# Laying the weight matrices of a one-step decoder out in the order of their transfers

## The chip, the cores and the metric

The kernel runs on one NeuronCore of one Trainium2 chip. The metric is the device time of one execution in microseconds (us), as the median of several runs. A second number, the span, is the time from the first to the last instruction in the one execution that was taken with the hardware profiler; that execution has a time of its own, which is given beside its span below.

The engines have short names throughout: PE is TensorE (its matmuls), PEld is TensorE's weight loading, DVE is VectorE, ACT is ScalarE, POOL is GpSimd, SP is SyncE. SP and POOL issue the transfers here; "SPq" is the time in which SP issues one. All transfers run on the core's 16 DMA engines.

## The reference

One step of a decoder layer for 256 prompt positions and 8 x 4 sampled positions, 288 columns in all, with a model width of 2048 and a feed-forward width of 5632, all in float32. Cut to what is computed:

```python
def ffn_half(h, g, wg, wu, wd):
    hn = rms_norm(h, g)
    return h + 0.5 * ((jax.nn.silu(hn @ wg) * (hn @ wu)) @ wd)

hp = ffn_half(hp, norm_ffn1, w_ffn1_gate, w_ffn1_up, w_ffn1_down)
cb, u, q, k, v, logf = mixer_in(hp, norm_mix, w_in, b_f)      # one projection of 6152 columns
conv_y = cb * short_conv(u_ext, conv_w)
attn_o = fox_prompt(q, k, v, logf)                            # causal, with forget gates
hp = mixer_out(hp, conv_y, attn_o, norm_conv_out, norm_attn_out, w_out)
hp = ffn_half(hp, norm_ffn2, w_ffn2_gate, w_ffn2_up, w_ffn2_down)
hp = ple_add(hp, p_prompt, norm_ple, w_ple_gate, w_ple_proj)
y_prompt = rms_norm(hp, norm_final)
```

The sampled positions go through the same layer, except that their attention (`fox_sample`) also reads 1024 past keys, values and forget gates of each of 8 sequences through a page table. The last 8 columns of `w_in` are the forget-gate weights.

## The kernel before, in words

**Weights.** Every large matrix is used in tiles of 512 rows by 256 columns (256 rows in a few down projections and in `w_ple_proj`). A tile of 512 rows is four blocks of 128 rows; row r of each block lies on partition r, so a partition holds four runs of 256 float32 (1 KB each) of one tile. `weight` (L270) names such a tile as a slice of the matrix, and `load_upto` (L237) issues its transfer on SP's queue (L242) into one of `RAW = 8` buffers of the pool `rawp`. The same eight buffers also take the pages of cached values, which POOL gathers (L250). `split_upto` (L257) then cuts a tile into halves of two blocks and splits each into a high and a low part: ACT writes `whi` (L265), DVE subtracts it to give `wlo` (L266), and there are `HALVES = 5` buffers of each. `pair` (L276) multiplies: for each block and each of two groups of 128 columns there are three matmuls (L298 to L300) with 288 moving columns. A half is therefore 12 matmuls, a tile 24.

**Order.** `steps` is a list of (transfers, function) that `run_steps` (L312) works off: before each step the loads of the next eight items are issued, then the function emits its instructions. Each engine executes what it was given in that order. A transfer on SP's queue waits, on SP, for its buffer to be released and for the eighth transfer before it on that queue to land, since eight semaphores are used in turn; everything behind it on SP waits with it.

**Small loads.** `small_loads` (L161, issued at L166) puts four transfers on SP's queue in the middle of the first feed-forward layer, behind seven loads of gains (L137): the forget-gate bias `bf`, the forget-gate weights `wf`, and the page table in two forms, `pidx` and `ptb`. `wf` is `w_in[:, 6144:6152]`: 2048 runs of 8 float32 (32 bytes). From `ptb`, DVE makes `idx` (L167), the row numbers for all gathers. Behind them on SP come the next weight tiles.

**Keys and values.** `k_turn` (L461, with `k_fetch` L456) gathers one page of keys with POOL (`kg`, L458), transposes it on DVE (`kt`, L467) and stores it with POOL to DRAM (`KD`, L469); 64 pages are spread over the first feed-forward layer. During the mixer, `k_scores` reads them back (`KT<-KD`, L247) and multiplies (L726). `v_round` gathers four pages of values for each of 16 rounds (L250) and multiplies them (L783). `prompt_head` (L822) has POOL load a row of forget sums, `bk`, and wait for it before its next instruction (L824).

Of the kernel before, what the change touches and what calls it, by code (L numbers as in the profile page):

```python
# [25 lines left out]
P = 128  # L26
D = 2048
KT = D // P
# [6 lines left out]
NH = 8  # L35
# [53 lines left out]
def build(nc, tc, ctx, A, O):  # L89
# [3 lines left out]
    v, s, g, pe, sy = nc.vector, nc.scalar, nc.gpsimd, nc.tensor, nc.sync  # L93
# [23 lines left out]
    cols = A["consts"].shape[1]  # L117
# [3 lines left out]
    def const(name):  # L121
        r, a, b = CONST_COLS[name]
        return C[:r, a:b]
# [32 lines left out]
    wf = cst.tile([P, KT, NH], F32, name="wf")  # L156
# [3 lines left out]

    def small_loads():  # L161
        for to, src in ((bf, A["b_f"].rearrange("(h o) -> h o", o=1)),
                        (wf, A["w_in"][:, 6144:6152].rearrange("(k p) c -> p k c", p=P)),
                        (pidx, A["page_table"].rearrange("b (g o) -> (b g) o", o=1)),
                        (ptb, A["page_table"].rearrange("b g -> (b g)").partition_broadcast(P))):
            tc.keep_in_program_order(sy.dma_start(to, src))  # L166
        v.tensor_scalar(idx, ptb, float(P), const("iota"), ALU.mult, ALU.add)  # L167
# [69 lines left out]
    def load_upto(n):  # L237
        while state["loaded"] < min(n, len(items)):
            it = items[state["loaded"]]
            if it["kind"] == "w":  # L240
                t = rawp.tile([P, it["nk"], 256], F32, name="wraw", tag="raw")
                d = sy.dma_start(t, it["src"].rearrange("(k p) c -> p k c", p=P))  # L242
                if state["used"] < 24:
                    tc.keep_in_program_order(d)
            elif it["kind"] == "k":
                t = W["kt"][0].tile([P, 2, 4, NH, 32], F32, name="KT", tag="KT", bufs=3)
                sy.dma_start(t.rearrange("p a i h r -> p (a i h r)"), it["src"])  # L247
            else:
                t = rawp.tile([P, NH * P], F32, name="page", tag="raw")
                g.indirect_dma_start(out=t, out_offset=None, in_=it["src"],  # L250
                                     in_offset=bass.IndirectOffsetOnAxis(ap=it["rows"], axis=0))
            it["tile"] = t
            state["loaded"] += 1
# [14 lines left out]
            state["split"] += 1  # L268

    def weight(src, k0, nk, c0):  # L270
        return dict(kind="w", src=src[k0 * P:(k0 + nk) * P, c0:c0 + 256], nk=nk, parts={})

    def page(src, j):
        return dict(kind="p", src=src, rows=idx[:, j:j + 1])
# [1 line left out]
    def pair(src, c0, kts, act, evac, k_of=lambda k: k, late=0, tag="mm"):  # L276
# [4 lines left out]
        for ci, ks in enumerate(chunks):  # L281
            it = weight(src, ks[0], len(ks), c0)

            def fn(ci=ci, ks=ks, it=it):
                if ci == 0:
                    st["ps"] = [bank(tag, BANKS[tag]) for _ in range(2)]
                last = ci == len(chunks) - 1
                split_upto(state["halves_used"] + HALVES)
                state["chunk"] += 1
                for b in range(2):  # L290
                    o = st["ps"][b][:, :NT]
                    for j, k in enumerate(ks):
                        hi, lo = it["parts"][j // 2 * 2]
                        w = slice(b * P, b * P + P)
                        xh, xl = act(k_of(k))
                        f = ci == 0 and j == 0
                        l = last and j == len(ks) - 1
                        pe.matmul(o, hi[:, j % 2, w], xh, start=f, stop=False)  # L298
                        pe.matmul(o, hi[:, j % 2, w], xl, start=False, stop=False)  # L299
                        pe.matmul(o, lo[:, j % 2, w], xh, start=False, stop=l)  # L300
                    if b == 0:
                        run_deferred()
                    if last and late:
                        defer(lambda b=b, o=o: evac(b, o), late)
                    elif last:
                        evac(b, o)
                state["halves_used"] += len(ks) // 2

            out.append(([it], fn))
        return out  # L310

    def run_steps():  # L312
        for its, _ in steps:
            items.extend(its)
            for it in its:
                if it["kind"] == "w":
                    halves.extend((it, j) for j in range(0, it["nk"], 2))
        for its, fn in steps:
            load_upto(state["used"] + RAW)
            fn()  # L320
            state["used"] += len(its)
# [150 lines left out]
    def later_loads():  # L472
        t = load_gains(["norm_mix", "norm_ffn2", "norm_ple", "norm_final", "norm_conv_out", "norm_attn_out", "conv_w"], 16, sy)
        small_loads()
        defer(lambda: turn_gains(*t), 20)
# [17 lines left out]
    for c in range(4):  # L493
        xin.append(x_load(2 * c))
        xin.append(x_load(2 * c + 1))
        load_upto(c + 1)
# [662 lines left out]
]  # L1159


# [19 lines left out]
```

## Time and profile before

| | us |
|---|---|
| median of 3 runs | 2389.52 |
| lowest, highest | 2389.41, 2391.86 |
| the profiled execution, its own time | 2396.56 |
| its span | 2394.7 |
| PE busy in the span | 2365.7 |
| DVE, ACT, POOL busy | 1430.9, 1055.6, 498.6 |
| mean granted TensorE clock | 0.995 |
| DMA traffic | 510.84 MB in 410703 packets |

"Busy" is the union of an engine's instructions; a matmul's end is modelled, so a busy PE is not proof of full speed. In the rows by stage, `(x412)` is the number of instructions that started in the stretch, `PEclk` the granted share of TensorE's clock, and the last two columns are the mean busy share of the 16 DMA engines and what they moved in GB/s. In the wait rows, the columns are the total, the number of waits and the longest one. Queue q1 carries what SP issues, q0 what POOL issues.

### The profile page before, as it was taken

How to read it: one execution, taken by the hardware profiler on the slowest of the kernel's cores; microseconds unless marked ns; L12 is line 12 of the kernel's file. 1: busy time of each engine (PE TensorE's matmuls, PEld its weight loads, DVE VectorE, ACT ScalarE, POOL GpSimd, SP SyncE). 2: the span in 40 equal slices, each digit the busy share in tenths (PEclk: the TensorE clock that was granted, in tenths of full speed). 3: DMA queues.
4: the chain of work that ended last, by engine and by line, in shares of the span. 5: the costliest groups of instructions: out<-in, count | busy, mean ns of one | idle time of the engine just before them, and what ended most of it. 6: DMA issues, size and time to landing. Idle time of an engine off the chain costs nothing.

```text
span 2394.7 us, 46026 instructions
## 1 busy us (share of the span) xinstructions
PE 2365.7 (99%) x17856; PEld 2294.7 (96%) x17856; DVE 1430.9 (60%) x2588; ACT 1055.6 (44%) x1858; POOL 498.6 (21%) x688
## 2 busy tenths in 40 slices
PE   8999999999999999999999999999999999999997
PEld 8999999999999999888878899999999999999997
DVE  6556666666655585455456675555555555555765
ACT  5434443444444453333234454444444444444654
POOL 2025354353400011112545310000000000000100
PEclk9999999999999999999999999999999999999998
DMA  7478889898865556987887654545555555555542
GB/s 224 151 247 290 292 281 329 274 310 283 285 227 167 165 166 191 317 306 253 276 292 266 233 167 150 177 153 180 163 165 167 164 163 168 165 161 167 160 158 81
DMA packets 410703, 510.84 MB, mean 213 GB/s; under 512 B 22236, under 2 KB 379316, under 8 KB 406356
## 3 DMA queue, kind: packets, MB, share of 16 engines
q1 hardware_dynamic: 376596, 401.43, 52.4%
q0 software_dynamic: 33664, 106.13, 12.9%
q8 instruction: 140, 2.29, 0.4%
q14 instruction: 79, 0.65, 0.1%
q10 hardware_dynamic: 224, 0.34, 0.1%
HBM read 469.19 MB, written 38.63 MB: 212 GB/s over the span
## 4 chain that ended last, share of the span: by engine, by line
PE 93%; DMA 4%; issue 1%; DVE 1%; POOL 1%; ACT 0%; SPq 0%; POOLq 0%; DVEq 0%; ACTq 0%
PE mm L298 29%; PE mm L300 29%; PE mm L299 28%; DMA page<-in_cache_v_dram,idx 1%; PE va L726 1%; PE va L783 1%; PE va L298 1%; PE va L300 1%; PE va L299 1%; DMA wraw<-in_w_in_dram 1%; DMA bk<-FP 0%; POOL page L250 0%; DMA kg<-in_cache_k_dram,idx 0%; DMA wraw<-in_w_out_dram 0%; DMA xa<-in_x_prompt_dram 0%
## 5 line engine op out<-in xcount | busy, mean ns | idle before, releaser
L266 DVE TENSOR_TENSOR wlo<-wraw,whi 128x512 fp32r<-128x512 f32 x1384 | 967.5, 704 | 737.1 <-ACT whi L265 690.6
L265 ACT ACTIVATE whi<-wraw 128x512 fp32r<-128x512 f32 x1384 | 864.5, 630 | 989.0 <-PE mm L299 915.0
L298 PE MATMUL mm<-xh,whi 128*128 128x288 f32 x3712 | 1109.0, 299 | 0.8 <-DVE tg L358 0.8
L300 PE MATMUL mm<-xh,wlo 128*128 128x288 f32 x3712 | 1093.1, 295 | 3.6 <-DVE wlo L266 3.6
L299 PE MATMUL mm<-xl,whi 128*128 128x288 f32 x3712 | 1096.5, 295 | 0.0
L298 PEld LDWEIGHTS mm<-xh,whi 128*128 128x128 f32 x3712 | 697.1, 188 | 23.3 <-ACT whi L265 14.5
L300 PEld LDWEIGHTS mm<-xh,wlo 128*128 128x128 f32 x3712 | 700.1, 189 | 4.2 <-DVE wlo L266 4.2
L299 PEld LDWEIGHTS mm<-xl,whi 128*128 128x128 f32 x3712 | 698.3, 188 | 0.1
L298 PE MATMUL mm<-hh,whi 128*128 128x288 f32 x1408 | 416.8, 296 | 0.0
L299 PE MATMUL mm<-hl,whi 128*128 128x288 f32 x1408 | 415.4, 295 | 0.0
L300 PE MATMUL mm<-hh,wlo 128*128 128x288 f32 x1408 | 414.0, 294 | 0.0
L362 POOL TENSOR_TENSOR sr<-sg,rs 128x288 f32<-128x288 f32 x88 | 72.8, 828 | 1126.8 <-ACT sg L360 1126.7
L300 PEld LDWEIGHTS mm<-hh,wlo 128*128 128x128 f32 x1408 | 265.1, 188 | 0.0
L299 PEld LDWEIGHTS mm<-hl,whi 128*128 128x128 f32 x1408 | 264.3, 188 | 0.0
L298 PEld LDWEIGHTS mm<-hh,whi 128*128 128x128 f32 x1408 | 263.8, 187 | 0.0
L469 POOL DMA_DIRECT2D KD<-kt x256 | 142.5, 562 | 80.6 <-DVE kt L467 60.6
L230 POOL TENSOR_TENSOR acc<-acc,sq 128x288 f32<-128x288 f32 x66 | 57.1, 865 | 267.1 <-ACT sq L229 222.7
L380 DVE SCALAR_TENSOR_TENSOR h<-mm,h 128x288 f32<-128x288 f32 x192 | 86.7, 453 | 21.3 <-PE mm L300 20.8
L467 DVE STREAM_TRANSPOSE kt<-kg 128x1024 f32<-128x1024 f32 x64 | 79.2, 1238 | 29.0 <-DMA kg<-in_cache_k_dram,idx 22.3
L458 POOL DMA_INDIRECT kg<-in_cache_k_dram,idx x64 | 71.6, 1118 | 74.5 <-DMA wraw<-in_w_ffn_gate_dram 55.5
L360 ACT ACTIVATE sg<-tg 128x288 f32<-128x288 f32 x88 | 39.1, 445 | 104.7 <-DVE tg L358 104.7
L369 ACT ACTIVATE hh<-hd 128x288 fp32r<-128x288 f32 x88 | 39.2, 445 | 96.3 <-DVE hd L367 96.3
(294 smaller groups left out, 1544.0 us busy)
## 6 DMA issues: line engine op xcount, KB each, us to landing
wraw<-in_w_ffn_gate_dram SPq DMA_DIRECT2D x176, 512.0 KB, 3.7
wraw<-in_w_ffn_up_dram SPq DMA_DIRECT2D x176, 512.0 KB, 3.6
wraw<-in_w_ffn_down_dram SPq DMA_DIRECT2D x160, 512.0 KB, 3.6
wraw<-in_w_in_dram SPq DMA_DIRECT2D x96, 512.0 KB, 4.9
KD<-kt POOLq DMA_DIRECT2D x256, 128.0 KB, 5.6
KT<-KD SPq DMA_DIRECT2D x32, 1024.0 KB, 7.3
wraw<-in_w_out_dram SPq DMA_DIRECT2D x32, 512.0 KB, 4.4
wraw<-in_w_ple_gate_dram SPq DMA_DIRECT2D x32, 512.0 KB, 3.6
```

The costliest lines, as they stand in the source:

```text
L230: (v if k >= KT - last_on_v else g).tensor_tensor(acc, acc, sq, ALU.add)
L265: s.activation(hi, x, AF.Copy)
L266: v.tensor_tensor(lo, x, hi.bitcast(F32), ALU.subtract)
L298: pe.matmul(o, hi[:, j % 2, w], xh, start=f, stop=False)
L299: pe.matmul(o, hi[:, j % 2, w], xl, start=False, stop=False)
L300: pe.matmul(o, lo[:, j % 2, w], xh, start=False, stop=l)
L362: g.tensor_tensor(r, u, rs, ALU.mult)
L369: s.activation(H["hi"][:, k, :], t, AF.Copy)
L380: v.scalar_tensor_tensor(h[:, k, :], o, 0.5, h[:, k, :], ALU.mult, ALU.add)
L458: g.indirect_dma_start(out=KG[j], out_offset=None, in_=A["cache_k"], in_offset=bass.IndirectOffsetOnAxis(ap=idx[:, j:j + 1], axis=0))
L467: v.transpose(t, KG.pop(j).rearrange("p (h d c) -> p d h c", d=4, c=32))
L469: g.dma_start(KD[j // 2, :, j % 2, i].rearrange("(d c) n -> c d n", c=32), t[32 * i:32 * i + 32].rearrange("c d h r -> c d (h r)"))
```

## The change

The host lays each large matrix out anew. A matrix of R rows and C columns becomes an array of shape (C/256, 128, R/128, 256): all tiles of one group of 256 columns together, in them one partition after the other, and in a partition its blocks in order. What a partition needs for one tile is then one run of 4 KB (2 KB for a tile of 256 rows). Runs of neighbouring partitions are 16 KB apart for matrices of 2048 rows, 44 KB for the down projections of 5632 rows, and 2 KB for `w_ple_proj`. The forget-gate columns become an array of their own, `w_f`, of 128 rows of 512 bytes. The work on the host is not part of the device time.

```diff
-                        (wf, A["w_in"][:, 6144:6152].rearrange("(k p) c -> p k c", p=P)),
+                        (wf, A["w_f"]),
...
-                d = sy.dma_start(t, it["src"].rearrange("(k p) c -> p k c", p=P))
+                d = sy.dma_start(t, it["src"])
...
-        return dict(kind="w", src=src[k0 * P:(k0 + nk) * P, c0:c0 + 256], nk=nk, parts={})
+        return dict(kind="w", src=src[c0 // 256, :, k0:k0 + nk, :], nk=nk, parts={})
...
+def packed(w):
+    rows, cols = w.shape
+    return np.ascontiguousarray(w.reshape(rows // P, P, cols // 256, 256).transpose(2, 1, 0, 3))
...
+    host["w_f"] = np.ascontiguousarray(host["w_in"][:, 6144:].reshape(KT, P, NH).transpose(1, 0, 2))
+    host["w_in"] = host["w_in"][:, :6144]
+    for name in [n for n in host if n.startswith("w_") and n != "w_f"]:
+        host[name] = packed(host[name])
```

The instructions of each engine, their order and their waits stay as they were; the SP queue carries the same transfers in the same places, with other source shapes.

## The prediction

> **What bounds the kernel now.** I read the page's busy times first, then the busy times by stage, then TensorE's waits, and last the few places where those waits stand.
>
> ```profile
> span 2394.7 us, 46026 instructions
> PE 2365.7 (99%) x17856; PEld 2294.7 (96%) x17856; DVE 1430.9 (60%) x2588; ACT 1055.6 (44%) x1858; POOL 498.6 (21%) x688
> ...
> DMA packets 410703, 510.84 MB, mean 213 GB/s; under 512 B 22236, under 2 KB 379316, under 8 KB 406356
> ...
> wraw<-in_w_ffn_gate_dram SPq DMA_DIRECT2D x176, 512.0 KB, 3.7
> ...
> wraw<-in_w_ffn_down_dram SPq DMA_DIRECT2D x160, 512.0 KB, 3.6
> ```
> ```profile
> 0.00:45.00 45.00, 38.94 (x226) 33.42 (x227) 29.73 (x66) 26.74 (x56) 14.19 (x19) 1.00 0.77 244
> 130.00:160.00 30.00, 25.60 (x176) 24.67 (x175) 14.71 (x24) 9.10 (x15) 6.25 (x8) 0.89 0.68 218
> 160.00:885.00 725.00, 725.00 (x5427) 725.00 (x5426) 469.84 (x730) 326.33 (x562) 251.67 (x369) 1.00 0.79 259
> 1140.00:1345.00 205.00, 201.60 (x1464) 164.39 (x1463) 113.48 (x282) 75.94 (x160) 98.53 (x120) 1.00 0.84 285
> 1430.00:2260.00 830.00, 830.00 (x6227) 830.00 (x6226) 462.77 (x764) 372.92 (x637) 46.66 (x58) 1.00 0.52 165
> ```
>
> PE is busy for 2365.7 of 2394.7 us. In the two long stages it never stops: 6227 matmuls in 830 us are 0.1333 us each, and 5427 in 725 us are 0.1336, although the DMA engines are busy at 0.52 in one stage and 0.79 in the other. There a tile (24 matmuls, 3.2 us) is fetched eight tiles ahead, and its landing after 3.7 us is hidden. So the change can only act where PE waits:
>
> ```profile
> PE mm L412 <- DMA xa<-in_x_prompt_dram: 4.6, 1, 4.6
> PE mm L300 <- DVE wlo L266: 3.6, 2, 3.2
> PE va L783 <- DMA page<-in_cache_v_dram,idx: 3.1, 3, 1.6
> PE kt L182 <- DVE acc L230: 3.0, 1, 3.0
> PE kt L412 <- DMA xa<-in_x_prompt_dram: 1.4, 1, 1.4
> PE mm L298 <- DVE tg L358: 0.8, 1, 0.8
> ```
>
> The 3.0 us are the last norm, with no transfer in it; the 4.6 us are the first transfers of all, which go ahead of every weight. That leaves three places: the start (1.4 us), a stall near 151 us (3.6 and 0.8 us), and the rounds of cached values (3.1 us). The second has a tail, the lowered clock:
>
> ```profile
> 150.00:154.00 4.00, 1.55 (x12) 1.32 (x10) 1.10 (x1) 0.63 (x1) 0.57 (x1) 0.96 0.91 329
> 154.00:158.00 4.00, 2.82 (x10) 2.44 (x10) 3.60 (x6) 0.00 (x0) 1.74 (x3) 0.50 0.86 311
> 158.00:162.00 4.00, 3.23 (x14) 2.91 (x13) 3.46 (x6) 2.04 (x4) 2.19 (x3) 0.50 0.72 213
> 162.00:166.00 4.00, 4.00 (x26) 4.00 (x25) 2.15 (x3) 1.18 (x2) 3.70 (x7) 0.76 0.90 263
> ```
>
> 62 matmuls started in these 16 us where 120 fit at 0.1333 us: 58 too few are 7.7 us, of which 4.4 are the waits (3.6 + 0.8) and 3.3 the half clock.
>
> **The change, part by part.** *Weight packets.* Four packets of 1 KB become one of 4 KB. Nothing of q1 has 4 KB packets now, but POOL's gathers on q0 do. Two stretches where one queue had the engines nearly alone:
>
> ```profile
> DMA packets 572, 0.57 MB, mean 378 GB/s; under 512 B 18, under 2 KB 572, under 8 KB 572
> ...
> q1 hardware_dynamic: 571, 0.57, 108.5%
> ```
> ```profile
> DMA packets 633, 2.25 MB, mean 410 GB/s; under 512 B 65, under 2 KB 89, under 8 KB 633
> ...
> q0 software_dynamic: 607, 2.23, 100.9%
> ```
>
> The first is 1248.0 to 1249.5 us: 1.085 x 16 x 1500 / 571 = 46 ns per packet of 1 KB. The second is 1163.0 to 1168.5 us: 2.23 MB are 544 packets of 4096 bytes, so 1.009 x 16 x 5500 / 544 = 163 ns each, against 184 for four of the small ones. A tile (524,288 bytes) needs 1.39 us at 378 GB/s and 1.28 at 410, so 0.11 us less of all engines. In the long stages that is worth nothing: PE covers it. Without that cover every tile would show its 0.11 us.
>
> *The start.* The 1.4 us wait is for an `xa` issued just behind the first weight tile on one queue. It gains that tile's 0.11 us; at most 0.45, if all four tiles among the `xa` count; below, 0, as PE has other work within 0.5 us. I take 0.1.
>
> *The stall near 151 us.* The chain of waits and DVE's order of work:
>
> ```profile
> 132.58 4.66 DMA wraw<-in_w_ffn_up_dram
> 137.25 0.27 SPq L166
> 137.56 0.40 SPq L166
> 138.01 1.15 SPq L166
> 139.21 0.58 SPq L166
> ```
> ```profile
> 144.33 0.26 DVE L167 TENSOR_SCALAR idx<-ptb,consts 128x64 int32<-128x64 int32 x1 [4.58 <-DMA ptb<-in_page_table_dram]
> 144.50 1.89 DVE L266 TENSOR_TENSOR wlo<-wraw,whi 128x512 fp32r<-128x512 f32 x3
> 152.90 1.25 DVE L467 STREAM_TRANSPOSE kt<-kg 128x1024 f32<-128x1024 f32 x1 [6.51 <-DMA kg<-in_cache_k_dram,idx]
> 154.07 0.65 DVE L266 TENSOR_TENSOR wlo<-wraw,whi 128x512 fp32r<-128x512 f32 x1
> ```
>
> SP issues `bf`, `wf`, `pidx`, `ptb` in that order; `ptb` gives `idx`, `idx` releases the key gathers, and DVE, in order, waits 6.51 us for the first gathered page while the next `wlo` stands behind that wait. PE runs out meanwhile. Two things come earlier. First, `bf` starts when the transfer issued at 132.58 lands after 4.66 us; its tile saves 0.11. Second, the issue behind `wf` takes 1.15 us, the three others 0.27 to 0.58. `wf` now has 2048 packets of 32 bytes, and will have 128 of 512. I price its neighbour at 0.40, so `ptb` is issued 0.75 us earlier. The queue itself:
>
> ```profile
> DMA packets 2016, 0.06 MB, mean 32 GB/s; under 512 B 2016, under 2 KB 2016, under 8 KB 2016
> ...
> q1 hardware_dynamic: 2016, 0.06, 54.8%
> ```
>
> From 138 to 140 us these packets took 0.548 x 2 = 1.1 us of the engines; 128 packets even at 46 ns take 0.37. This overlaps the issue and I don't add it. Index and gather thus move up by 0.85 us. Bounds: 1.6 with the queue's 0.7 added; below, a loss of the 0.9 derived next.
>
> *Turns between the queues.* From 1234.0 to 1236.5 us both queues had work:
>
> ```profile
> q0 software_dynamic: 216, 0.80, 79.4%
> q1 hardware_dynamic: 220, 0.22, 25.0%
> ```
>
> 216 packets against 220, but 0.80 MB against 0.22: the engines alternate packet by packet, and the small weight packets leave POOL's gathers four fifths of the bytes. With 4 KB packets a gather gets half. One gather is 8 packets on each engine: 8 x (163 + 46) = 1.67 us beside a full weight queue now, 8 x (163 + 163) = 2.61 then, 0.9 us more. Against that, no byte is added: weights that overtake a gather are out of the way sooner. At 151 us two weight tiles run beside the first gather, so I let this take back 0.15 of the 0.85: 0.7 us. All later DVE work shifts with it; the clock I let drop as before.
>
> *The rounds of values.* There SP issues weight tiles in bursts of three (the first of them shown), ahead of the pages that PE then waits for:
>
> ```profile
> 1156.60 1.69 SPq L242 DMA_DIRECT2D wraw<-in_w_in_dram  x3
> ```
> ```profile
> PEld va L783 <- DMA page<-in_cache_v_dram,idx: 8.9, 8, 2.5
> ```
>
> Three tiles pass 0.33 us sooner. PE itself waited for pages 3 times, its weight loads 8 times; between them I take 5 late pages: 5 x 0.33 = 1.6 us. Bounds: 3.1, all of PE's waits, and a loss of 5 x 0.9 = 4.5 if the gathers lose their turns.
>
> *Sum.* 0.1 + 0.7 + 1.6 = 2.4 us less. The profiled execution, 2396.56 us (span 2394.7 and 1.9 around it), would become 2394.2. It is 7.0 us above the median of 2389.52, so a median run may hold less of these stalls than the profile shows; I carry the same 2.4 over, to 2387.1, and let the range pay for that.
>
> **The rivals.** *The stall nearly closes* (0.35). The clock fell only after a wait of 3.2 us, while page waits of up to 1.6 left it at 1.00:
>
> ```profile
> 152.00:154.00 2.00, 0.00 (x0) 0.00 (x0) 1.10 (x1) 0.00 (x0) 0.00 (x0) 0.92 0.99 390
> ```
>
> A mean of 0.92 over 2 us is 0.32 us at half clock, so it fell at 153.7, 2.3 us into the wait. If the wait shrinks below that, the 3.3 us of half clock go too; with the upper bounds of the index (0.9 more) and the pages (1.5 more) the gain is 8.1 us: 2381.4. For it speaks that 0.9 us off the wait (3.2 less 2.3) would do; against it, that my own shift is 0.7. The Trainium skill, "TensorE: Matmul & The Clock Gate", Part 1, has the clock go to half after at least one idle window of about 3.4 us; the trace saw it go 2.3 us into a wait. By that rule any shortening would keep the clock, and 3.3 us would join the sum: 5.7.
>
> *The gathers lose their turns* (0.12, slower). Place: key gathers at 148 us, pages from 1140 to 1345. Price: 0.9 us per gather that has the weight queue beside it all the way; five late pages and the one at 151 us, 6 x 0.9 = 5.4, less the 0.1 of the start: 2394.8. It decides once weights stay queued for a whole gather, as at 1234 us. Against it: from 1163.0 to 1168.5, ahead of a late page, q0 had the engines alone.
>
> *Hidden anyway* (0.10). In unprofiled runs the stalls may be short enough for nothing to be left: 2389.5, within 1 us.
>
> *Strided rows collide* (0.03, slower). Partitions now lie 16 KB apart. Were weights to move at half of 378 GB/s, the stage from 160 to 885 us would need 165/189 + 94/410 = 1.10 of the engines: 0.10 x 725, about 72 us more, 2462. Against it: down projections already step by 8 KB, also a power of two, and land in 3.6 us beside 3.7. The Trainium skill, "DMA: Bandwidth & Descriptors", section "Latency and other measured facts", warns of row pitches at large powers of two, with loss from 2 MiB on; no run here shows it.
>
> **How the numbers follow.** The forecast, a gain of 1 to 4.8 us, has 0.40. About 0.2%, 4.8 us, is what a measurement of this kernel can tell from no change. Faster by more: 0.35 plus 0.03 from the forecast's edge, 0.38. Slower by more: 0.12 and 0.03, less 0.03 for gathers that lose only part, 0.12. The rest, 0.50, is within. The forecast's own range is 2384.7 to 2388.5; for 8 in 10 I go from 2379.0, past the first rival, to 2391.5, which holds the hidden case and the highest run.
>
> **What would show it.** Right: the DMA packets of the span, 410703 before, fewer by some 265,000 (by the shapes, 672 tiles of 512 rows lose 384 packets each, 40 of 256 rows lose 128, `wf` 1920); the issue behind `wf` near 0.4 us; `idx` near 143.5; DVE's wait for `kg` ending near 152; PE's waits for pages below 3.1 us in total; 0.133 us a matmul in the long stages as before. Wrong: page waits above 3.1 us (turns), no half clock after 150 us (first rival), tiles landing later than 3.7 us (strides).

## The result, and the profile after

The changed kernel took 2399.32 us (median of 6 runs, 2394.22 to 2401.91) against 2390.89 (6 runs, 2389.41 to 2394.0) for the kernel before: a ratio of 1.0026, 95% interval 1.0015 to 1.0038. The prediction was 2387.1, from 2379.0 to 2391.5. The kernel became slower, by 0.26%, and the interval (0.15% to 0.38%) leaves out both a gain and no change. A second batch of 11 runs gave 1.0026 again (1.0017 to 1.0035).

The page of the changed kernel, its head, one queue and two kinds of weight tiles (the last column is the median from issue to landing, in us):

```profile
span 2392.2 us, 46026 instructions
...
DMA packets 145615, 510.84 MB, mean 214 GB/s; under 512 B 20188, under 2 KB 23092, under 8 KB 141268
...
q1 hardware_dynamic: 111508, 401.43, 52.3%
...
wraw<-in_w_ffn_gate_dram SPq DMA_DIRECT2D x176, 512.0 KB, 4.2
...
wraw<-in_w_ffn_down_dram SPq DMA_DIRECT2D x160, 512.0 KB, 3.7
```

The same queue in the kernel before:

```profile
q1 hardware_dynamic: 376596, 401.43, 52.4%
```

265,088 packets fewer, as the shapes say, and nothing gained by it: the queue took 52.3% of the DMA engines' span for the same bytes, where it had taken 52.4%. And a tile of the gate weights lands after 4.2 us, not 3.7. This execution, 2394.22 us, is the fastest of its six, and the one shown of the kernel before, 2396.56, was slower than any of the six runs of it here, so their spans say the opposite of the medians. The rows that speak for the changed kernel come from a profile of the second batch (2399.71 us, span 2397.8), here called "the changed kernel again" (e1). TensorE's waits there:

```profile
PE mm L412 <- DMA xa<-in_x_prompt_dram: 4.5, 2, 4.3
PE va L783 <- DMA page<-in_cache_v_dram,idx: 4.1, 6, 2.4
PE mm L300 <- DVE wlo L266: 4.0, 1, 4.0
```

The waits stand where they stood. The two that were to shrink are longer: 4.1 us for pages (3.1 before) and 4.0 in one piece near 151 us (3.2 the longest before). In the first profile after, the fastest of its six, they are 3.8 and 2.2 us: pages were late there too, but the other wait was shorter than before. The operations of TensorE that multiply the cached values, in the kernel before, in the first profile after, and again; the columns are count, shortest, median and longest in ns, and the start of the first and the last:

```profile
L783 PE MATMUL va<-page,PT x256: 592/592/617, 1145.2 to 1337.4; 128*32 128x512 f32 x128
```
```profile
L783 PE MATMUL va<-page,PT x256: 592/593/617, 1143.1 to 1335.5; 128*32 128x512 f32 x128
```
```profile
L783 PE MATMUL va<-page,PT x256: 592/592/1062, 1143.4 to 1340.9; 128*32 128x512 f32 x128
```

The rounds of values last 192.2, 192.4 and 197.5 us. In the last row one matmul took 1062 ns, nearly twice as long as the shortest: the clock fell once within the rounds. The first profile after has nothing of this, so one kernel's rounds differ by 5.1 us between two executions. The stretch in which it did, in e1:

```profile
1254.00:1258.00 4.00, 1.60 (x6) 0.18 (x2) 2.71 (x7) 2.77 (x8) 3.18 (x4) 0.85 0.66 200
1258.00:1262.00 4.00, 3.40 (x11) 0.55 (x10) 0.00 (x0) 0.00 (x0) 0.25 (x1) 0.50 0.93 347
```

17 matmuls start in these 8 us, where the long stages start 60 in the same time, with the clock at 0.85 and 0.50, while the DMA engines are at last busy (0.93) with the pages that are waited for.

### The profile page after: what moved, and what is told of

Its sections match the earlier page's. It is cut to its first block, busy times and chain, and to the rows that moved or that the text cites. A ratio compares the mean times of both kernels' runs of the same rounds, so it can differ in the third digit from the quotient of the medians.

```text
span 2392.2 us, 46026 instructions
## 1 busy us (share of the span) xinstructions
PE 2364.2 (99%) x17856; PEld 2293.6 (96%) x17856; DVE 1431.9 (60%) x2588; ACT 1055.7 (44%) x1858; POOL 499.0 (21%) x688
## 3 DMA queue, kind: packets, MB, share of 16 engines
q1 hardware_dynamic: 111508, 401.43, 52.3%
## 4 chain that ended last, share of the span: by engine, by line
PE 95%; DMA 2%; DVE 1%; issue 1%; POOL 0%; ACT 0%; POOLq 0%; DVEq 0%
PE mm L298 30%; PE mm L300 29%; PE mm L299 29%; PE va L726 1%; PE va L783 1%; DMA page<-in_cache_v_dram,idx 1%; PE va L298 1%; PE va L300 1%; PE va L299 1%; DMA kg<-in_cache_k_dram,idx 0%; DMA bk<-FP 0%; DMA wraw<-in_w_in_dram 0%; PE kt L206 0%; POOL page L250 0%; DMA wraw<-in_w_ffn_gate_dram 0%
```

## The experiments

Each kernel was timed beside the kernel before, in four batches: e1 to e4, e5 to e8, e9 to e12, e13 to e16. The ratio is to the kernel before in the same batch. Diffs are against the changed kernel, but for e4 and what is built on it (e11, e15), which start from the kernel before. "Stall" is the time that DVE waited for the first gathered keys (the wait near 151 us), "rounds" the time from the first to the last start of the values' matmuls; both are of the one profiled execution, so that a difference of a few us is read only where several kernels agree on it. "The pitch" is the distance between the runs of neighbouring partitions in DRAM.

| kernel | median us (runs) | ratio, 95% interval | stall us | rounds us |
|---|---|---|---|---|
| before, its profile | | 1 | 6.9 | 192.2 |
| the changed kernel, its first profile | 2399.32 (6) | 1.0026, 1.0015 to 1.0038 | 6.5 | 192.4 |
| e1 changed, again | 2397.99 (11) | 1.0026, 1.0017 to 1.0035 | 8.2 | 197.5 |
| e2 4 KB packets, a tile one run | 2391.25 (11) | 0.9996, 0.9987 to 1.0005 | 4.3 | 193.2 |
| e3 1 KB packets, 16 KB pitch | 2392.27 (11) | 0.9998, 0.9989 to 1.0007 | 3.8 | 196.6 |
| e4 w_f alone | 2390.09 (11) | 0.9989, 0.9980 to 0.9998 | 6.8 | 191.7 |
| e5 4 KB packets, 20 KB pitch | 2393.36 (12) | 1.0005, 0.9996 to 1.0014 | 6.0 | 190.9 |
| e6 w_in, w_out and w_f | 2394.96 (11) | 1.0011, 1.0002 to 1.0020 | 5.4 | 197.1 |
| e7 feed-forward, per-layer input, w_f | 2394.53 (11) | 1.0013, 1.0004 to 1.0022 | 8.1 | 192.4 |
| e8 changed, bk ahead | 2393.60 (11) | 1.0006, 0.9997 to 1.0015 | 8.2 | 193.0 |
| e9 1 KB packets, a block one run | 2391.73 (12) | 0.9995, 0.9987 to 1.0004 | 6.0 | 191.1 |
| e10 changed, early keys | 2397.95 (12) | 1.0027, 1.0017 to 1.0038 | moved | 194.5 |
| e11 w_f, early keys, bk ahead | 2386.94 (12) | 0.9976, 0.9968 to 0.9985 | moved | 186.3 |
| e12 e2, early keys, bk ahead | 2388.90 (12) | 0.9981, 0.9973 to 0.9990 | moved | 185.1 |
| e13 e7 with 20 KB pitch | 2390.36 (12) | 0.9995, 0.9986 to 1.0004 | 4.5 | 191.7 |
| e14 changed, early keys, bk ahead | 2392.92 (11) | 1.0004, 0.9992 to 1.0016 | moved | 192.7 |
| e15 w_f, bk ahead | 2385.79 (7) | 0.9974, 0.9963 to 0.9985 | 6.3 | 186.3 |
| e16 e2, bk ahead | 2386.16 (9) | 0.9978, 0.9968 to 0.9987 | 5.0 | 186.3 |

### What in the layout costs: e1 to e4

e1 is the changed kernel, unaltered.

> The changed kernel as it is, for a second trace and a closer interval. The trace that came with it was its fastest execution of six (2394.22 us against a median of 2399.32), so it cannot show where a median execution loses 8 us. Turns: the loss stands in the rounds of cached values (1140 to 1345 us) and near 150 us, as waits for pages and key pages above the 3.8 us and 2.2 us of that first trace; the stage from 1430 to 2260 us keeps 6227 matmuls in 830 us. Strides (partitions 16 KB apart): the packets of 4 KB average well above 159 ns, their shortest, as in the first trace, also where q1 has the engines alone. Moved small loads: the loss stands near 150 us alone. Ratio to before 1.002 to 1.004.

e2 keeps packets of 4 KB, but lays a tile's 128 partitions next to each other, 4 KB apart, so that a tile is one run of 512 KB:

```diff
-        return dict(kind="w", src=src[c0 // 256, :, k0:k0 + nk, :], nk=nk, parts={})
+        flat = src[c0 // 256, k0:k0 + nk, :].rearrange("k x -> (k x)").rearrange("(p y) -> p y", p=P)
+        return dict(kind="w", src=flat, nk=nk, parts={})
...
+    x = w.reshape(blocks, P, cols // 256, 256).transpose(2, 1, 0, 3)
...
+        [x[:, :, a:b].reshape(cols // 256, b - a, P * 256) for a, b in zip(starts, ends)], 1))
```

> Packets of 4 KB as in the change, but every tile one run of 512 KB: neighbouring partitions are 4 KB apart instead of 16 KB (44 KB for the down projections). Strides: packets average near 163 ns, as POOL's gathers had, gate tiles land in under 3.7 us, and the time is at or below before (ratio 0.997 to 1.000). Turns: nothing changes, ratio 1.002 to 1.004. Moved small loads: the same ratio as the change.

e3 keeps the partitions 16 KB (44 KB) apart, but puts the four blocks of a tile 4 KB (11 KB) apart within the partition's row, so that the packets are of 1 KB:

```diff
-        return dict(kind="w", src=src[c0 // 256, :, k0:k0 + nk, :], nk=nk, parts={})
+        at, step, n = places(src.shape[2])[k0]
...
+        return dict(kind="w", src=src[c0 // 256, :, at:at + step * (nk - 1) + 1:step, :], nk=nk, parts={})
...
+        return {4 * n: (n, 4, 4) for n in range(4)}
```

> The changed layout with its 16 KB (44 KB) between partitions, but the four blocks of a tile lie 4 KB (11 KB) apart in each partition, so that a tile moves in packets of 1 KB again. Turns: the gathers get their four fifths back, ratio 0.998 to 1.001. Strides: as slow as the change or slower, ratio 1.002 or more, with packets of 1 KB averaging above the 51.8 ns of before. Moved small loads: the same ratio as the change.

e4 is the kernel before with the contiguous `w_f`:

```diff
-                        (wf, A["w_in"][:, 6144:6152].rearrange("(k p) c -> p k c", p=P)),
+                        (wf, A["w_f"]),
```

> The kernel before with the forget-gate weights alone laid out as rows of 512 bytes. Moved small loads: all of the loss, ratio 1.002 to 1.004. Turns and strides: no loss; the index comes 0.75 us sooner, ratio 0.999 to 1.000.

`w_f` alone is worth 0.11%, so the rest of the change costs not 0.26% but 0.37% (1.0026 less 0.9989). Neither the large packets alone (e2) nor the pitch alone (e3) gives that: they stand 0.07% and 0.09% above e4, no more than the scatter, and so neither the turns nor the strides of the expectations hold by themselves. The place differs, though, as the issues in the rounds show (1140 to 1345 us; count, size, median to landing); first e4, then e1, the first profile after, e2 and e3:

```profile
wraw<-in_w_in_dram SPq DMA_DIRECT2D x27, 512.0 KB, 6.8
...
page<-in_cache_v_dram,idx POOLq DMA_INDIRECT x58, 6.1
```
```profile
wraw<-in_w_in_dram SPq DMA_DIRECT2D x27, 512.0 KB, 6.5
...
page<-in_cache_v_dram,idx POOLq DMA_INDIRECT x58, 7.2
```
```profile
wraw<-in_w_in_dram SPq DMA_DIRECT2D x27, 512.0 KB, 6.1
...
page<-in_cache_v_dram,idx POOLq DMA_INDIRECT x58, 6.0
```
```profile
wraw<-in_w_in_dram SPq DMA_DIRECT2D x27, 512.0 KB, 5.3
...
page<-in_cache_v_dram,idx POOLq DMA_INDIRECT x57, 6.1
```
```profile
wraw<-in_w_in_dram SPq DMA_DIRECT2D x27, 512.0 KB, 4.9
...
page<-in_cache_v_dram,idx POOLq DMA_INDIRECT x56, 6.7
```

With the pitch, pages land after 7.2 (e1, 4 KB packets) and 6.7 us (e3, 1 KB); without it after 6.1 (e2), in the same 4 KB packets. But the changed kernel's first profile has 6.0 with the pitch, and e16, without it, 6.5, so one landing time proves little. The rounds of all kernels say more. Where POOL still waits for `bk`, they last 192.4 to 197.5 us in the five profiles with the 16 KB pitch in `w_in` (the first after, e1, e3, e6, e10) and 190.9 to 193.2 in the seven others; where `bk` is loaded ahead, 192.7 and 193.0 (e14, e8) against 185.1 to 186.3 (e11, e12, e15, e16). The one that overlaps is the changed kernel's fastest execution. So in the rounds the pitch decides, and the packet size hardly matters, as far as e3, the one kernel with the pitch and 1 KB packets, shows. The fallen clock is not the mark of it: e2 has a matmul of 1062 ns there too.

At the stall both are needed, as DVE's wait for the keys shows, in e1, e2 and e3:

```profile
DVE kt L467 <- DMA kg<-in_cache_k_dram,idx: 8.2, 1, 8.2
```
```profile
DVE kt L468 <- DMA kg<-in_cache_k_dram,idx: 4.3, 2, 3.5
```
```profile
DVE kt L469 <- DMA kg<-in_cache_k_dram,idx: 3.8, 1, 3.8
```

e3's rounds are as long as e1's, but its stall is 4.4 us shorter, which fits its ratio being below e1's. The time from the start of the index to the first transposed page shows the same: 8.5, 10.3, 10.2 and 10.3 us in the four profiles with 4 KB packets at 16 KB in the feed-forward weights (the first after, e1, e7, e8), 7.0 to 8.6 in the ten others that keep the order of the small loads. What this costs TensorE depends on what it is compared with: from 110 to 170 us 391 matmuls start in e1, 428 in e2, 436 in e3, but only 393 in e4. At 0.133 us each e1 is 5 to 6 us behind e2 and e3 there, and 0.3 behind e4, whose profiled execution was the slowest of its eleven.

### Which matrices: e6 and e7

e6 has the new layout for `w_in` and `w_out` alone, e7 for the feed-forward and per-layer-input weights alone, both with `w_f`; the other matrices are read as before, except that `w_in` in e7 has rows of 24,576 bytes, its forget-gate columns being gone, and not of 24,608:

```diff
+        if len(src.shape) == 2:
+            part = src[k0 * P:(k0 + nk) * P, c0:c0 + 256].rearrange("(k p) c -> p k c", p=P)
+        else:
+            part = src[c0 // 256, :, k0:k0 + nk, :]
...
-    for name in [n for n in host if n.startswith("w_") and n != "w_f"]:
...
+    for name in ("w_in", "w_out"):
```

(e7: `for name in [n for n in host if n.startswith("w_ffn") or n.startswith("w_ple")]`.)

> The new layout for w_in and w_out alone, with the new forget-gate array; the feed-forward and last matrices as before. Two places: the stall near 151 us behaves as in the kernel with the new forget-gate array alone, the loss of some 5 us in the rounds of cached values stays: ratio 1.000 to 1.002 (0.999 plus 5 in 2390). One place only (near 151 us): ratio 0.999. Diffuse loss: in between, with no stage to show it.

> The new layout for the feed-forward and last matrices alone, with the new forget-gate array; w_in and w_out as before. Two places: the stall near 151 us stays long (excess over the full pace some 8 us) and the rounds of cached values are as before: ratio 0.999 to 1.001. One place only (near 151 us): the whole loss, ratio 1.002 or more. Place in the rounds of values only: ratio 0.999.

Against e4, e6 loses 0.22% and e7 0.24%; together 0.46%, where e1 loses 0.37%, the same within the intervals. The places separate: e6 has the long rounds (197.1) and a short stall (5.4), e7 the long stall (8.1) and rounds as before (192.4). The ratio of e7 was not foreseen, though: 1.0013 is above what two places asked for (to 1.001) and below one place (1.002).

### Whether it is the power of two: e5 and e13

e5 gives every row of a partition in the matrices of 2048 rows four blocks that are not used, so that partitions lie 20 KB apart; the packets stay at 4 KB. e13 does the same to e7.

```diff
...
+    if rows == 2048:
+        x = np.concatenate([x, x[:, :, :4]], 2)
```

> The changed kernel with four unused blocks behind the 16 of each partition, so that neighbouring partitions lie 20 KB apart instead of 16 KB; packets stay 4 KB. Power of two: the loss goes, ratio 0.999 to 1.000, gate and ple_gate tiles land near 3.6 to 3.8 us as with whole-tile runs. Scatter of any kind (only a tile in one run is fast): ratio stays at 1.002 to 1.003 and tiles land at 4.0 us or more.

> The FFN's and the per-layer input's weights in the new layout with a pitch of 20 KB instead of 16 KB (four blocks of every row left unused; the down projections keep 44 KB), w_in and w_out as before, w_f contiguous. Theory 'pitch and packet size together': of e7's 1.0013 most goes, 0.999 to 1.0005. Rival 'the size of the FFN's packets alone': 1.001 to 1.002, as e7, with the first gather of the keys as late as there (the first transpose waiting 8 us for kg).

Against e1, e5's rounds went from 197.5 to 190.9, and its ratio from 1.0026 to 1.0005; against e7, e13's stall went from 8.1 to 4.5 and its ratio from 1.0013 to 0.9995. e7 and e13 read the same `w_in`, so that cannot be what e7 lost by. But e5 did not quite reach what was expected (0.999 to 1.000): it takes back 0.21 of the 0.37% and stays 0.16% above e4, with rounds and a stall no longer than there. Where that rest is lost its one profile does not show.

The stage from 1430 to 2200 us shows the pitch with nothing beside it, as SP's weights are there alone on the engines. Issues of the kernel before, of the first profile after, of e13, and of e3 (1 KB packets with the pitch):

```profile
wraw<-in_w_ffn_gate_dram SPq DMA_DIRECT2D x80, 512.0 KB, 3.5
wraw<-in_w_ffn_down_dram SPq DMA_DIRECT2D x72, 512.0 KB, 3.5
```
```profile
wraw<-in_w_ffn_gate_dram SPq DMA_DIRECT2D x80, 512.0 KB, 4.0
...
wraw<-in_w_ffn_down_dram SPq DMA_DIRECT2D x73, 512.0 KB, 3.5
```
```profile
wraw<-in_w_ffn_gate_dram SPq DMA_DIRECT2D x79, 512.0 KB, 3.6
wraw<-in_w_ffn_down_dram SPq DMA_DIRECT2D x74, 512.0 KB, 3.3
```
```profile
wraw<-in_w_ffn_gate_dram SPq DMA_DIRECT2D x80, 512.0 KB, 3.9
...
wraw<-in_w_ffn_down_dram SPq DMA_DIRECT2D x73, 512.0 KB, 4.1
```

In packets of 4 KB a tile lands after 4.0 us at 16 KB, after 3.6 at 20 KB (gate), and after 3.3 to 3.5 at 44 KB (down). In e2, with 4 KB between partitions, gate tiles land after 3.5. So of the pitches tried with these packets only 16 KB is slow, and a power of two alone is not: 4 KB is one too. Nor is it the pitch alone: in e3 the down tiles, 44 KB apart but in packets of 1 KB that lie 11 KB apart, land after 4.1. The Trainium skill, "DMA: Bandwidth & Descriptors", section "Latency and other measured facts", lists row pitches at large powers of two: 207 GB/s at 512 KiB, 164 at 2 MiB, and full rate again once 4 MiB was padded by 4 KiB. Here the remedy agrees (4 KB more), but the onset does not: the later landing is there at 16 KB. The memory channels, which the page offers as an unverified reason, no run here shows.

### Small packets without the pitch: e9

A block of 128 rows by 256 columns is one run of 128 KB here, partitions 1 KB apart; packets are of 1 KB:

```diff
-        return dict(kind="w", src=src[c0 // 256, :, k0:k0 + nk, :], nk=nk, parts={})
+        return dict(kind="w", src=src[c0 // 256, k0:k0 + nk].rearrange("k p c -> p k c"), nk=nk, parts={})
...
-    return np.ascontiguousarray(w.reshape(rows // P, P, cols // 256, 256).transpose(2, 1, 0, 3))
+    return np.ascontiguousarray(w.reshape(rows // P, P, cols // 256, 256).transpose(2, 0, 1, 3))
```

> The layout's unit is a block of 128 rows by 256 columns, one run of 128 KB: a packet is 1 KB again and a tile's rows of one partition lie 128 KB apart, but neighbouring partitions lie 1 KB apart instead of 16 KB. Theory 'turns and pitch together': with small packets POOL's gathers keep their turns, and without the pitch there is nothing dear in a packet; the ratio is that of e2_tile_run or of the kernel with w_f alone, 0.998 to 1.000, the waits near 151 us and in the rounds of values no longer than before. Rival 'the pitch alone': the same. Rival 'turns are what costs in e2 too, only hidden by its cheaper packets': below e2's 0.9996 by 0.1% or more, 0.998. Rival 'any new place of the weights costs': 1.002 and more.

0.9995, as e2 (0.9996): without the pitch it makes no difference to the time whether a packet has 1 or 4 KB.

### Taking the waits away: e8, e10 to e12, e14 to e16

e8 loads the row `bk` one head ahead into a second buffer, so that POOL no longer stands at L824 for it:

```diff
+    def bk_load(hh):
+        M["bk"] = W["vp"][0].tile([P, SEQ], F32, name="bk", tag="bk", bufs=2)
+        g.dma_start(M["bk"], FP[hh, :].partition_broadcast(P))
...
-        g.dma_start(bk, FP[hh, :].partition_broadcast(P))
+        bk = M.pop("bk")
...
+        if hh < NH - 1:
+            bk_load(hh + 1)
...
+        bk_load(0)
```

> The changed kernel with the row of forget sums of each head loaded one head ahead into a second buffer, so that POOL no longer stands at it with page gathers behind. If the loss in the rounds of values comes through POOL standing at that small transfer, held up behind weight packets: its waits of 27 to 33 us nearly vanish, pages are issued sooner, and some 5 us come back, ratio 1.000 or below. If pages are late because their own packets are slow: ratio 1.001 to 1.003.

e10 moves the small loads ten steps up and issues the first three gathers of keys when their buffers open:

```diff
-        for i in range(3) if j == 0 else (j + 2,):
-            if i < DB * PAGES:
-                k_fetch(i)
+        if 0 < j < DB * PAGES - 2:
+            k_fetch(j + 2)
...
-    steps.insert(44, ([], later_loads))
+    steps.insert(34, ([], later_loads))
...
-    steps.insert(46, ([], lambda: opened("kg", "right")))
+    steps.insert(46, ([], lambda: (opened("kg", "right"), [k_fetch(i) for i in range(3)])))
```

> The changed kernel with the loads of the later small tables ten steps earlier and the first three gathers of the keys issued as soon as their buffers open, so that the stall near 151 us has nothing to wait for. Theory 'two places': of the 0.26% lost (0.4% against w_f alone) the part near 151 us goes, and more, as that stall cost 8 us in the kernel before too: ratio 0.998 to 1.000, TensorE's idle time from 130 to 160 us down by 5 us or more, the rounds of values as in e1_again. Rival 'the rounds of values are all of it': ratio 1.001 to 1.003, though the stall is gone, with more lost in the rounds of values.

e11 puts both edits on e4, e12 on e2, e14 on the changed kernel. e15 is e4 with e8's edit alone, e16 is e2 with it.

> The kernel before with the contiguous w_f alone, the early small loads and gathers of e10, and the row bk loaded one head ahead as in e8. If the two places are waits on small transfers and not bandwidth, both go: ratio 0.995 to 0.998. If what is taken out at the one comes back at the other, 0.999 to 1.000.

> The same two edits on the layout of e2_tile_run (each tile one run of 512 KB). Theory 'the small loads set it': as e11 within 0.1%, 0.995 to 0.998, for the weights are nowhere late. Rival 'larger packets still take turns': above e11 by 0.1% or more.

> The changed kernel with both edits of e10 and e8: small loads and first gathers early, bk one head ahead. Theory 'two places and nothing else': as e11 within 0.1%, 0.997 to 0.999. Rival 'dear packets cost elsewhere too' (e10 moved its stall to 128 and 490 us): 1.000 to 1.002.

> The kernel before with the contiguous w_f and bk one head ahead, the small loads where they were. Theory 'bk is worth it by itself, the early small loads nothing' (as e10 against e1_again): as e11 within 0.1%, 0.997 to 0.9985. Rival 'both are worth something': 0.9985 to 0.9995.

> The layout of e2_tile_run with bk one head ahead, the small loads where they were. Theory 'bk by itself': as e12 within 0.1%, 0.9975 to 0.999. Rival 'both': 0.999 to 1.000.

e10 did not do what was expected of it. Its stall went from 152 us, but not away; DVE's order of work in e10:

```profile
122.93 0.45 DVE L380 SCALAR_TENSOR_TENSOR h<-mm,h 128x288 f32<-128x288 f32 x1
129.34 1.25 DVE L466 STREAM_TRANSPOSE kt<-kg 128x1024 f32<-128x1024 f32 x1 [5.96 <-DMA kg<-in_cache_k_dram,idx]
130.51 0.42 DVE L380 SCALAR_TENSOR_TENSOR h<-mm,h 128x288 f32<-128x288 f32 x1
```

The transposes moved up with the gathers, and DVE now stands 5.96 us for them at 123 us, with a result of the down projection (`h`) behind that wait, which TensorE then waits for:

```profile
PE mm L298 <- DVE h L380: 2.9, 1, 2.9
```

Two waits for DVE behind it, 1.9 us together and the longer one near 490 us, are new as well. With the 2.9 that makes 4.8 us, and 4.8 is what TensorE waited near 151 us in e1 (4.0 and 0.8). So the wait changed its place and not its size. That e15 is as fast as e11, and e16 as e12, says the same: the early keys bring nothing. And e16 against e15 (0.9978 and 0.9974) says that the larger packets bring nothing either, where they do no harm.

The row `bk` is another matter. POOL in e1, then in e15:

```profile
1241.52 0.60 POOL L822 DMA_DIRECT2D bk<-FP  x1
1242.12 0.84 POOL L886 TENSOR_TENSOR tC<-tC,rs 128x288 f32<-128x288 f32 x1
1250.05 0.76 POOL L824 TENSOR_TENSOR pm<-consts,bk 128x128 f32<-128x128 f32 x1 [7.08 <-DMA bk<-FP]
...
1252.62 1.29 POOL L250 DMA_INDIRECT page<-in_cache_v_dram,idx  x1 [0.16 <-issue]
```
```profile
1248.33 0.59 POOL L821 DMA_DIRECT2D bk<-FP  x1 [0.25 <-DVE pst L847]
1248.94 0.43 POOL L827 TENSOR_TENSOR pm<-consts,bk 128x128 f32<-128x128 f32 x1
```

POOL waited 7.08 us for the row, and the next pages were issued behind that wait. With the row ahead, the rounds are shorter: by 5.4 us on e4 (e15), 6.9 on e2 (e16), and 4.5 on the changed kernel (e8) against e1, though not against the first profile after (192.4). But it is a wait of the kernel before, not one that the change made: POOL waits 29.4 us in all for these rows before and 29.6 in e1, and in the rounds the changed layout stays behind without the wait too, 193.0 against 186.3 and 186.3. e14 shows that best: 1.0004, with the same two edits that bring e11 to 0.9976, where 0.997 to 0.999 was expected if the two places were all. So the gain of e8 (1.0006, between its two expectations) is not the loss being found; it comes on top of it.

e15 beats both kernels: 2385.79 us, 0.26% below the kernel before and, from the ratios, 0.5% below the changed one.

## Why the prediction was wrong

**The price of a packet failed, and so did what it was to buy.** The 163 ns of a 4 KB packet were POOL's gathers', and I gave them to weight packets 16 KB apart. In the rounds, by queue rows of the kernel before, of e1 and of e2:

```profile
q1 hardware_dynamic: 24779, 24.62, 37.1%
```
```profile
q1 hardware_dynamic: 6424, 23.42, 33.8%
```
```profile
q1 hardware_dynamic: 7093, 25.84, 34.7%
```

0.371 x 16 x 205 us over 24.62 MB are 49.4 us of engine time per MB, 0.338 x 16 x 205 over 23.42 are 47.3: 4% less, not the 11% of 163 against 184. Over the whole span there was no saving. The 0.11 us per tile, on which three terms of the sum rested, was not there, and tiles of the 16 KB pitch landed up to 0.5 us later instead.

The price itself was not wrong, its place was: e2, with the same packets and no pitch, takes 44.0 us per MB in the rounds, the 11%, and e5, e12 and e16 by the same working 44.1 to 45.1, where the six profiles with 4 KB packets at 16 KB in `w_in` have 47.3 to 48.6. Even so the second step failed there too, from a cheaper tile to a shorter wait: e2 is no faster than e4 (0.9996 and 0.9989), nor e16 than e15 (0.9978 and 0.9974).

**The wrong rival was dismissed.** The sign named for it, tiles landing later than 3.7 us, came: 4.2 for the gate weights. "Strided rows collide" had a chance of 0.03 because the down projections' old step of 8 KB cost nothing. That row was for packets of 1 KB whose neighbours on other partitions lay 8 KB apart; it didn't show 4 KB packets 16 KB apart, where e2, e5 and e13 find the loss. Its size was wrong too: the long stages hid it, as the prediction's own cover says (0.133 us a matmul from 1430 to 2260 us, unchanged), so it cost some 0.37% and not 72 us. The two places where it shows are those where gathers run beside weights.

**"The gathers lose their turns"** came nearest in time (2394.8, slower; the ratio on the median shown gives 2395.7), and in e1 one of its rows came true: pages land 1.1 us later (7.2 against 6.1 in e4), where 0.9 was priced; in the first profile after they do not (6.0). Its reason is at most half right, and its nearness in time is partly luck. e2 has the same 4 KB packets and lands its pages after 6.1. Large packets are needed for the longer stall (e1 against e3: 8.2 and 3.8), which turns would explain but no run shows by itself, and they cost nothing without the pitch.

**The start** (0.1) can't be told from the scatter: its wait was 1.4 before, 1.3 after, 1.8 in e1 and 1.1 in e4.

**The stall near 151 us.** Its first half was right, its second wrong. `pidx` took 0.55 us to issue, where 1.15 was to become 0.40, and the index came earlier; the issue in the first profile after, and DVE there and in e1:

```profile
L166 SPq DMA_DIRECT2D pidx<-in_page_table_dram x1: 550/550/550, 136.8 to 136.8; - x1
```
```profile
142.16 0.25 DVE L167 TENSOR_SCALAR idx<-ptb,consts 128x64 int32<-128x64 int32 x1 [3.61 <-DMA ptb<-in_page_table_dram]
...
150.68 1.25 DVE L467 STREAM_TRANSPOSE kt<-kg 128x1024 f32<-128x1024 f32 x1 [6.46 <-DMA kg<-in_cache_k_dram,idx]
```
```profile
141.93 0.26 DVE L167 TENSOR_SCALAR idx<-ptb,consts 128x64 int32<-128x64 int32 x1 [3.66 <-DMA ptb<-in_page_table_dram]
...
152.24 1.25 DVE L467 STREAM_TRANSPOSE kt<-kg 128x1024 f32<-128x1024 f32 x1 [8.25 <-DMA kg<-in_cache_k_dram,idx]
```

The index is 2.2 and 2.4 us earlier, more than the 0.85, as this includes an earlier start. From index to transpose it was 8.6 us before, 8.5 in the first profile and 10.3 in e1: the gather gave back up to 1.7 us where I had charged 0.15. By itself the contiguous `w_f` gains 0.11% (0.02% to 0.20%), some 2.6 us, where 0.75 was priced; which wait gives more than the price, the one profile of e4 does not tell.

**The rounds of values** (1.6 us gained) lost 5.8 in e1 against e4, and 0.7 in the first profile after. The lower bound, a loss of 4.5, was near, but its reason was turns.

**Settled and open.** Settled by e2, e5 and e13: with packets of 4 KB it is the 16 KB pitch that makes the kernel slower; without it 0.21 to 0.30 of the 0.37% is back (e5, e2), and of e7's 0.24% three quarters (e13). Open: why the pitch slows a tile, where the rest of e5's loss is, and what else e7 loses. Its stall is 1.3 us longer than in e4, while its ratio is 0.24% (5.7 us) worse. Between the two profiled executions, 2397.13 and 2393.83 us, the difference is 3.3 us, and most of it stands at the start: 219 matmuls had started by 45 us in e7, 235 in e4, 2.1 us at 0.133 each. But e1 had started 237, so the layout does not do that in every execution. That e4's profiled execution was the slowest of its 11 may be part of the rest.

## What to carry to other kernels

Fewer, larger packets are worth something only where transfers set the time: e2 took 11% less engine time per MB in the rounds and was no faster. A layout that is contiguous in each partition can still put the partitions at a bad distance: 16 KB in packets of 4 KB cost 0.37% here. A tile as one run took back 0.30 of that, a row padded by one tile's part 0.21. When a change moves only bandwidth, look at the transfers that share the engines with it, not at those it makes cheaper.

## What the hardware showed that was not expected

A pitch of 16 KB between partitions, in packets of 4 KB, lands a 512 KB tile 0.5 us later (4.0 against 3.5), with no other traffic, while the queue's share of the engines hardly changes: 52.3% and 52.4% of the span.

The length of a wait does not tell when the clock falls. The prediction took 2.3 us into a wait as the point. Worked out in the same way, from the mean clock in windows of 2 us, the clock fell 2.0 us into the wait near 151 us in the first profile after and 2.3 in e7, but in e1 only 4.2 us after the start of a wait of 4.0 us, when the wait was over, and in e8 after 4.6. Shorter waits do not settle it either. e16 and e13 at the same stall, waits first, then the clock in 156 to 160 us (the third column from the end):

```profile
PE mm L301 <- DVE wlo L266: 1.8, 2, 1.6
PE mm L299 <- DVE tg L359: 1.3, 1, 1.3
```
```profile
156.00:160.00 4.00, 3.54 (x26) 3.54 (x27) 3.79 (x7) 2.45 (x5) 2.82 (x4) 1.00 0.73 231
```
```profile
PE mm L302 <- DVE tg L362: 1.3, 1, 1.3
PE mm L304 <- DVE wlo L266: 1.2, 1, 1.2
```
```profile
156.00:160.00 4.00, 4.00 (x23) 4.00 (x22) 2.58 (x3) 1.43 (x3) 3.84 (x7) 0.67 0.81 193
```

In e13 waits of 1.2 and 1.3 us brought it to 0.67; in e16 waits of 1.6 and 1.3 us, their ends 2.1 us apart as in e13, left it at 1.00. So two short waits close to each other can do what the prediction asked of one long wait, and need not; what decides between them no run here shows. The rival "the stall nearly closes", which set its price by that point, had no such point: the first profile after has 2.2 us there, below it, and lost the clock all the same. The Trainium skill, "TensorE: Matmul & The Clock Gate", Part 1, has the clock go to half after at least one idle window of about 3.4 us, by which any shortening would have kept it; these rows don't bear that out, at 2.2 us in one piece, or 2.5 us in two.
